# Scaling the forgetting-attention probabilities on GpSimd in place of ScalarE

## The chip, the core and the metric

The kernel runs on one core of a Trainium2 chip. A core has four engines that matter here: TensorE (PE in the profile, with its weight loads as PEld), VectorE (DVE), ScalarE (ACT) and GpSimd (POOL). A fifth, SyncE (SP), issues most DMAs. Each engine works through its own queue strictly in order and waits on semaphores for the others. The metric is the device time of one execution in microseconds (us), lower is better; what is compared is the median of several executions.

## What is computed

Two decoder layers, each: half a SwiGLU feed-forward, a token mixer, another half feed-forward. 512 tokens, model width 1024. The mixer has eight forgetting-attention (FoX) heads of width 64 and four differential-attention heads. For one block of 128 queries the FoX heads compute

```python
s_f = einsum('bhqd,bhkd->bhqk', qf, k_f) * scale_f
s_f = s_f + cf[..., :, None] - cum_f[..., None, :]
s_f = where(causal, s_f, -inf)
p_f = softmax(s_f, axis=-1)
o_f = einsum('bhqk,bhkd->bhqd', p_f, v_f)
```

The last step of that softmax is a division of each row by its sum. This is the step that the change touches.

## The kernel before, in words

**Precision.** Matrix products run in a split form: an operand is stored as a rounded high part and a low remainder, and three products replace one. `split` (lines 82 to 85) makes the parts: ScalarE copies the high part (L83), VectorE subtracts it from the source (L84). Both engines therefore work for TensorE throughout the program.

**The mixer.** Its attention is a list of twelve units, four differential heads and then eight FoX heads, each cut into four query blocks. The loop over `s` in `mixer` is a software pipeline: at step `s` it emits the softmax of one query block (`softmax_step`), the transposes of the probabilities of a unit five steps behind (`trans_step`), and the product with V six steps behind (`pv_step`). Between those, `fill_to` emits pieces of matrix products that do not depend on attention (projections for later heads, then the early part of the output projection); the table `TARGET` says how much filler has been emitted by each unit. The table runs flat toward the end, so the last FoX heads have little filler beside them.

**One FoX query block**, with `n` keys (128, 256, 384 or 512), goes through these lines:

1. TensorE computes the scores into PSUM (L821, L822) and adds the causal mask (L824).
2. VectorE adds the forget-gate row from a tile named `rope` in the profile (its buffer is reused), writes the result `e` into the probability tile `pg`, and takes the row minimum into `st` (L857). The signs are flipped, so the minimum plays the part of a maximum.
3. ScalarE computes the exponential in place and the row sum (L859, followed by a read of the accumulator).
4. VectorE takes the reciprocal of the row sum (L860), 128x1.
5. ScalarE multiplies the block in place by that reciprocal (L861).
6. TensorE transposes the probabilities (L871); ScalarE and VectorE split them into the two parts (L880, L881, tiles `pair` and `pt`); TensorE multiplies by V (L910, L911); ScalarE copies half of the result (L940, `fot`) and VectorE adds the other half (L941); L892 and L893 split the result into `y` for the output projection.

There are two `pg` tiles, one for even units and one for odd ones, so a unit's probabilities are overwritten two units later.

**Other work at the same time.** ScalarE and VectorE also split the keys and queries of the next heads (L770, L771, L758, L759, from `kdup` and `qk_t`), the output-projection weights into `XA` (L83, L84), and evict projections (L787).

**GpSimd** issues DMAs that add one weight block onto another (L134) in the feed-forward stages, casts a table once per mixer (L626), and multiplies four tiles at the very end of the program (L1144).

**What sets the order.** The code is written as one program; a scheduler walks it and gives each engine a fixed sequence, with its own estimate of how long each instruction takes. A change of engine for one operation can therefore move its neighbours.

Of the kernel before, what the change touches and what calls it, by code (L numbers as in the profile page):

```python
# [12 lines left out]
ALU = mybir.AluOpType  # L13
# [39 lines left out]
def trunk(ctx, tc, xT, x, gains, gain_row, w_gu, w_dn, w_in, w_ff, w_out, fbias, lams, subln, consts, rope, out):  # L53
    nc = tc.nc
    act, dve, pool, pe, sp = nc.scalar, nc.vector, nc.gpsimd, nc.tensor, nc.sync
# [524 lines left out]
    def mixer(l, n_next, mid):  # L580
# [14 lines left out]
        def pr_tile(u, qb):  # L595
            w = (qb + 1) * P
            return pg[u % 2][:, PR[qb]:PR[qb] + w]

        def pm_tile():
            return pg[nxt("pm", 2)][:, 1280:1792]  # L600
# [215 lines left out]
        def scores(q1, kk, m, qb, masked):  # L816
            n = (qb + 1) * P
            w = max(n, 256)
            p = psum("b")
            lq = q1[m][:, qb * P:n]  # L820
            pe.matmul(p[:, 0:w], lq, kk[m][:, 0, 0:w], start=True, stop=False)  # L821
            pe.matmul(p[:, 0:w], lq, kk[m][:, 1, 0:w], start=False, stop=not masked)  # L822
            if masked:
                pe.matmul(p[:, qb * P:n], identb, maskb, start=False, stop=True)  # L824
            return p
# [3 lines left out]
        def softmax_step(u, qb):  # L829
            kind, h = units[u]  # L830
            n = (qb + 1) * P
            st = sm.tile([P, 6], F32, tag="st", name="st", bufs=6)
            if kind == "d":
                q1, kk = qk[("d", h)]
                pm = []
                for m in range(2):
                    p = scores(q1, kk, m, qb, False)
                    e = pr_tile(u, qb) if m == 0 else pm_tile()
                    dve.tensor_tensor_reduce(out=e[:, 0:n], in0=p[:, 0:n], in1=maskw[:, S - n:S], op0=ALU.add,
                                             op1=ALU.min, scale=1.0, scalar=3.0e38, accum_out=st[:, m:m + 1])  # L840
                    act.activation(out=e[:, 0:n], in_=e[:, 0:n], func=AF.Exp, scale=-1.0, bias=st[:, m:m + 1],
                                   accum_out=st[:, 2 + m:3 + m])
                    pm.append(e)
                dve.reciprocal(out=st[:, 4:6], in_=st[:, 2:4])
                dve.tensor_tensor(out=st[:, 5:6], in0=st[:, 5:6], in1=nlam, op=ALU.mult)
                act.mul(out=pm[1][:, 0:n], in_=pm[1][:, 0:n], mul=st[:, 5:6])
                dve.scalar_tensor_tensor(out=pm[0], in0=pm[0], scalar=st[:, 4:5], in1=pm[1][:, 0:n],
                                         op0=ALU.mult, op1=ALU.add)
                probs[u].append(pm[0])
            else:  # L850
                q1, kk = qk[("f", h // 2)]
                if qb == 0:
                    cbs[h] = rope_t[h % 2]
                    sp.dma_start(out=cbs[h], in_=cum_d[h:h + 1, :].partition_broadcast(P))
                p = scores(q1, kk, h % 2, qb, True)
                e = pr_tile(u, qb)
                dve.tensor_tensor_reduce(out=e, in0=p[:, 0:n], in1=cbs[h][:, 0:n], op0=ALU.add, op1=ALU.min,  # L857
                                         scale=1.0, scalar=3.0e38, accum_out=st[:, 0:1])
                act.activation(out=e, in_=e, func=AF.Exp, scale=-1.0, bias=st[:, 0:1], accum_out=st[:, 2:3])  # L859
                dve.reciprocal(out=st[:, 4:5], in_=st[:, 2:3])  # L860
                act.mul(out=e, in_=e, mul=st[:, 4:5])  # L861
                probs[u].append(e)

        pts = {}
# [216 lines left out]
        for s in range(4 * len(units) + 5 + LAG):  # L1081
            u, i = divmod(s, 4)

            def pace(j):
                a = target[min(u, len(target) - 1)]
                b = target[min(u + 1, len(target) - 1)]
                fill_to(a + (b - a) * (3 * i + j) / 12)
            now, later[:] = list(later[:1]), later[1:]
            v, kb = divmod(s - 4 - LAG, 4)
            if 0 <= v < len(units):  # L1090
                trans_step(v, kb)
            pace(1)
            if u < len(units):
                softmax_step(u, i)
            pace(2)
            for f in now:
                f()
            v, kb = divmod(s - 5 - LAG, 4)
            if 0 <= v < len(units):
                pv_step(v, kb)  # L1100
            pace(3)
# [250 lines left out]
```

## Time and profile before

| | |
|---|---|
| median of 3 executions | 1886.66 us (1884.94 to 1890.23) |
| the profiled execution | 1887.3 us, of which the span from first to last instruction is 1885.2 us |
| mean granted TensorE clock | 0.992 of full speed |
| ScalarE busy over the whole span | 1139.6 us, 60% |
| VectorE busy | 1625.6 us, 86% |
| GpSimd busy | 129.0 us, 7% |
| FoX blocks, both mixers | 64, first L861 at 486.7 us, last at 1506.9 us |
| the multiplies at L861 alone | 387 to 737 ns, median 560 ns |

The profile gives each engine's busy time over the span and in windows of it, the groups of instructions by line, who waited for whom, and the chain of work that ended last, followed backwards from the end. The first mixer's FoX blocks run their multiplies from 486.7 to 582.1 us, the second mixer's from 1411.6 to 1506.9 us; the two stretches look alike, shifted by about 925 us. TensorE's busy time is modelled from pipelined matmuls, so overlapping matmuls count as busy even where the pace is lower; its weight-load time is the better measure of how much work it was given in a stretch.

### The profile page before, as it was taken

How to read it: one execution, taken by the hardware profiler on the slowest of the kernel's cores; microseconds unless marked ns; L12 is line 12 of the kernel's file. 1: busy time of each engine (PE TensorE's matmuls, PEld its weight loads, DVE VectorE, ACT ScalarE, POOL GpSimd, SP SyncE). 2: the span in 40 equal slices, each digit the busy share in tenths (PEclk: the TensorE clock that was granted, in tenths of full speed). 3: DMA queues.
4: the chain of work that ended last, by engine and by line, in shares of the span. 5: the costliest groups of instructions: out<-in, count | busy, mean ns of one | idle time of the engine just before them, and what ended most of it. 6: DMA issues, size and time to landing. Idle time of an engine off the chain costs nothing.

```text
span 1885.2 us, 24722 instructions
## 1 busy us (share of the span) xinstructions
PE 1837.5 (97%) x8814; PEld 1511.2 (80%) x8814; DVE 1625.6 (86%) x2537; ACT 1139.6 (60%) x1797; POOL 129.0 (7%) x156
## 2 busy tenths in 40 slices
PE   7999999999999999999999999999999999999997
PEld 5788888787877889888878988887788688888886
DVE  7799998878685989899998989997786869998988
ACT  6565546546786755565585556554577957455564
POOL 2000000000000000000001000000000000000101
PEclk8999999999999999999999999999999999999999
DMA  9676675243336576676647666643433367756842
GB/s 298 185 208 183 188 193 150 69 135 106 100 115 195 168 193 175 160 213 181 180 140 218 173 173 181 173 140 99 125 102 108 111 178 197 212 143 184 226 111 90
DMA packets 95962, 305.38 MB, mean 162 GB/s; under 512 B 12616, under 2 KB 15176, under 8 KB 95840
## 3 DMA queue, kind: packets, MB, share of 16 engines
q1 hardware_dynamic: 74960, 232.68, 36.7%
q0 software_dynamic: 19584, 69.21, 20.6%
q10 hardware_dynamic: 1296, 1.93, 0.3%
q8 instruction: 69, 1.13, 0.2%
q14 instruction: 53, 0.43, 0.1%
HBM read 289.03 MB, written 2.16 MB: 154 GB/s over the span
## 4 chain that ended last, share of the span: by engine, by line
PE 81%; DVE 10%; ACT 5%; DMA 2%; issue 1%; SPq 0%; DVEq 0%; ACTq 0%
PE ps_c L385 12%; PE ps_c L386 12%; PE ps_c L387 12%; PE ps L386 9%; PE ps L385 9%; PE ps L387 9%; PE ps_a L385 3%; PE ps_a L386 3%; PE ps_a L387 3%; DVE wg L84 3%; PE ps_t L487 2%; DVE x L516 1%; ACT pg L859 1%; DMA raw<-w_gu 1%; PE ps_b L871 1%
## 5 line engine op out<-in xcount | busy, mean ns | idle before, releaser
L83 ACT CAST wg<-raw 128x1024 fp32r<-128x1024 f32 (+1 forms) x533 | 545.2, 1030 | 492.0 <-PE ps_c L387 183.0
L84 DVE TENSOR_TENSOR wg<-raw,wg 128x1024 fp32r<-128x1024 f32 (+1 forms) x533 | 629.7, 1192 | 111.2 <-ACT wg L83 108.1
L385 PE MATMUL ps_c<-wg,xf 128*128 128x512 f32 (+1 forms) x768 | 287.6, 375 | 3.8 <-ACT xf L83 1.6
L386 PE MATMUL ps_c<-wg,xf 128*128 128x512 f32 (+1 forms) x768 | 286.4, 373 | 1.8 <-DVE wg L84 1.8
L387 PE MATMUL ps_c<-wg,xf 128*128 128x512 f32 (+1 forms) x768 | 284.9, 373 | 0.0
L385 PE MATMUL ps<-wg,xf 128*128 128x512 f32 (+1 forms) x576 | 219.2, 382 | 7.4 <-ACT wg L83 7.3
L386 PE MATMUL ps<-wg,xf 128*128 128x512 f32 (+1 forms) x576 | 216.2, 376 | 0.6 <-DVE wg L84 0.6
L387 PE MATMUL ps<-wg,xf 128*128 128x512 f32 (+1 forms) x576 | 215.1, 375 | 1.2 <-DVE xf L84 1.2
L385 PEld LDWEIGHTS ps_c<-wg,xf 128*128 128x128 f32 x768 | 145.3, 189 | 31.8 <-ACT xf L83 2.8
L386 PEld LDWEIGHTS ps_c<-wg,xf 128*128 128x128 f32 x768 | 145.6, 190 | 27.4 <-DVE wg L84 2.7
L387 PEld LDWEIGHTS ps_c<-wg,xf 128*128 128x128 f32 x768 | 144.9, 189 | 25.3 <-DVE xf L84 0.4
L134 POOL DMA_DIRECT2D raw<-w_gu x88 | 76.4, 868 | 1131.9 <-DMA raw<-w_gu 667.6
L385 PE MATMUL ps_c<-wg,hf 128*128 128x512 f32 x352 | 138.6, 394 | 4.4 <-DVE x L516 4.3
L386 PE MATMUL ps_c<-wg,hf 128*128 128x512 f32 x352 | 137.5, 391 | 0.0
L387 PE MATMUL ps_c<-wg,hf 128*128 128x512 f32 x352 | 137.3, 390 | 0.0
L385 PEld LDWEIGHTS ps<-wg,xf 128*128 128x128 f32 x576 | 110.1, 191 | 25.9 <-ACT wg L83 7.8
L387 PEld LDWEIGHTS ps<-wg,xf 128*128 128x128 f32 x576 | 109.6, 191 | 20.9 <-DVE xf L84 1.7
L386 PEld LDWEIGHTS ps<-wg,xf 128*128 128x128 f32 x576 | 110.1, 191 | 18.9 <-DVE wg L84 1.1
L516 DVE SCALAR_TENSOR_TENSOR x<-ps_c,x 128x512 f32<-128x512 f32 x192 | 124.3, 684 | 1.0 <-PE ps_c L387 0.9
L385 PE MATMUL ps_a<-XA,wg 128*128 128x512 f32 x256 | 106.9, 418 | 2.6 <-ACT XA L339 1.9
L386 PE MATMUL ps_a<-XA,wg 128*128 128x512 f32 x256 | 101.9, 398 | 2.5 <-DVE XA L340 2.5
L386 PE MATMUL ps<-wg,hf 128*128 128x512 f32 x264 | 103.2, 391 | 0.0
(274 smaller groups left out, 3516.1 us busy)
## 6 DMA issues: line engine op xcount, KB each, us to landing
raw<-w_gu SPq DMA_DIRECT2D x219, 512.0 KB, 4.3
raw<-w_dn SPq DMA_DIRECT2D x100, 512.0 KB, 3.6
raw<-w_gu POOLq DMA_DIRECT2D x88, 512.0 KB, 7.3
raw<-w_in SPq DMA_DIRECT2D x48, 512.0 KB, 3.4
raw<-w_dn POOLq DMA_DIRECT2D x40, 512.0 KB, 5.7
kdup<-qk_t SPq DMA_DIRECT2D x64, 128.0 KB, 2.3
raw<-w_out SPq DMA_DIRECT2D x16, 512.0 KB, 3.7
raw<-w_dn SPq DMA_DIRECT2D x20, 256.0 KB, 3.4
```

What stands on the lines that cost most here:

```text
L83: act.copy(out=hi, in_=src)
L84: dve.tensor_tensor(out=lo, in0=src, in1=rf(hi), op=ALU.subtract)
L134: pool.dma_start(out=t, in_=where(two, h)[1], accum_op=ALU.add)
L385: pe.matmul(p, lh, rh, start=start, stop=False, skip_group_check=again)
L386: pe.matmul(p, lh, rl, start=False, stop=False, skip_group_check=again)
L387: pe.matmul(p, ll, rh, start=False, stop=stop, skip_group_check=again)
L487: pe.transpose(pj[j][:, e * 256 + p * P:e * 256 + (p + 1) * P], hs[j][p][:, o:o + P], ident)
L516: dve.scalar_tensor_tensor(out=xc, in0=src, scalar=scale, in1=xc, op0=ALU.mult, op1=ALU.add)
L859: act.activation(out=e, in_=e, func=AF.Exp, scale=-1.0, bias=st[:, 0:1], accum_out=st[:, 2:3])
L871: pe.transpose(p[:, (qb - kb) * P:(qb - kb + 1) * P], probs[u][qb][:, kb * P:(kb + 1) * P], ident)
```

## The change

The in-place multiply of a FoX block by its reciprocal row sum leaves ScalarE and becomes a tensor-scalar multiply on GpSimd. The differential heads keep theirs (L846) on ScalarE. Nothing else in the source is edited.

```diff
 act.activation(out=e, in_=e, func=AF.Exp, scale=-1.0, bias=st[:, 0:1], accum_out=st[:, 2:3])
 dve.reciprocal(out=st[:, 4:5], in_=st[:, 2:3])
-act.mul(out=e, in_=e, mul=st[:, 4:5])
+pool.tensor_scalar(out=e, in0=e, scalar1=st[:, 4:5], scalar2=None, op0=ALU.mult)
 probs[u].append(e)
```

The scheduler moves other instructions with it, in the two FoX stretches only. On ScalarE, in the last FoX heads of the first mixer (`pg_2961` and `pg_2962` are the probability tiles of even and odd units), this stood in its queue before:

```order
L861 ACTIVATE pg_2962<-pg_2962,st 128x512
L859 ACTIVATE pg_2961,st<-pg_2961,st 128x128
L880 CAST pair<-ps_b 128x512
L861 ACTIVATE pg_2961<-pg_2961,st 128x128
L859 ACTIVATE pg_2961,st<-pg_2961,st 128x256
L940 COPY fot<-ps_b 64x512
L880 CAST pair<-ps_b 128x384
L859 ACTIVATE pg_2961,st<-pg_2961,st 128x384
L861 ACTIVATE pg_2961<-pg_2961,st 128x256
L880 CAST pair<-ps_b 128x256
```

and for the same head this stands there now:

```order
L859 ACTIVATE pg_2961,st<-pg_2961,st 128x128
L880 CAST pair<-ps_b 128x512
L859 ACTIVATE pg_2961,st<-pg_2961,st 128x256
L940 COPY fot<-ps_b 64x512
L880 CAST pair<-ps_b 128x384
L83 CAST XA_2950<-raw 128x1024
L880 CAST pair<-ps_b 128x256
L83 CAST XA_2955<-raw 128x1024
L859 ACTIVATE pg_2961,st<-pg_2961,st 128x384
L859 ACTIVATE pg_2961,st<-pg_2961,st 128x512
```

The multiplies are gone from between the exponentials and the splits, and two casts of the output-projection weights have come up into this head from later ones.

On GpSimd, around the first mixer, the queue held only the table cast and the weight DMAs before:

```order
L626 CAST tri<-tri_f 128x512
L134 DMA raw<-w_dn 128x1024
L134 DMA raw<-w_gu 128x1024 x8
L134 DMA raw<-w_dn 128x1024
L134 DMA raw<-w_gu 128x1024
```

Now the 32 multiplies of the eight FoX heads stand between; these are the last of them, with the DMAs of the next feed-forward behind:

```order
L861 TENSOR_SCALAR pg_2961<-pg_2961,st 128x512
L861 TENSOR_SCALAR pg_2962<-pg_2962,st 128x128
L861 TENSOR_SCALAR pg_2962<-pg_2962,st 128x256
L861 TENSOR_SCALAR pg_2962<-pg_2962,st 128x384
L861 TENSOR_SCALAR pg_2962<-pg_2962,st 128x512
L134 DMA raw<-w_gu 128x1024 x8
```

The DMAs of the next feed-forward stage now wait in line behind the last multiply.

On VectorE, in the last heads of the first mixer, the queue around the third `XA` split was before:

```order
L857 ISA pg_2961,st<-ps_b,rope 128x256
L857 ISA st 128x1
L84 TENSOR_TENSOR XA_2950<-raw,XA_2950 128x1024
L860 RECIPROCAL st<-st 128x1
L857 ISA pg_2961,st<-ps_b,rope 128x384
L857 ISA st 128x1
L881 TENSOR_TENSOR pair<-ps_b,pair 128x512
L860 RECIPROCAL st<-st 128x1
L941 TENSOR_TENSOR pg_2961<-ps_b,fot 64x512
```

and is now:

```order
L857 ISA pg_2961,st<-ps_b,rope 128x256
L857 ISA st 128x1
L84 TENSOR_TENSOR XA_2950<-raw,XA_2950 128x1024
L860 RECIPROCAL st<-st 128x1 x3
L857 ISA pg_2961,st<-ps_b,rope 128x384
L857 ISA st 128x1
L941 TENSOR_TENSOR pg_2961<-ps_b,fot 64x512
L84 TENSOR_TENSOR XA_2955<-raw,XA_2955 128x1024
L881 TENSOR_TENSOR pair<-ps_b,pair 128x512
```

Three reciprocals, which were spread out, now stand together behind the `XA` split, and the next `XA` split follows closely.

## The prediction

> **What bounds the kernel now.** I read the page first, for the share of each engine and the chain of work that ended last.
>
> ```profile
> PE 1837.5 (97%) x8814; PEld 1511.2 (80%) x8814; DVE 1625.6 (86%) x2537; ACT 1139.6 (60%) x1797; POOL 129.0 (7%) x156
> PE 81%; DVE 10%; ACT 5%; DMA 2%; issue 1%; SPq 0%; DVEq 0%; ACTq 0%
> ```
>
> Over the span TensorE is the bound, and ScalarE is only 60% busy. Taking work from it is worth nothing unless there is a place where it is late. The chain has 5% ScalarE, so I looked for that place with busy times by stage around the FoX heads.
>
> ```profile
> 486.00:540.00 54.00, 54.00 (x277) 43.60 (x276) 36.62 (x85) 38.39 (x76) 0.00 (x0) 1.00 0.31 98
> 540.00:560.00 20.00, 19.21 (x107) 14.45 (x105) 18.84 (x56) 19.11 (x48) 0.00 (x0) 1.00 0.51 146
> 560.00:580.00 20.00, 17.43 (x92) 12.71 (x93) 16.22 (x47) 19.84 (x50) 0.00 (x0) 1.00 0.18 60
> 1465.00:1485.00 20.00, 19.02 (x106) 14.40 (x104) 18.93 (x55) 19.13 (x48) 0.00 (x0) 1.00 0.52 146
> 1485.00:1505.00 20.00, 17.60 (x93) 12.87 (x94) 16.04 (x46) 19.84 (x51) 0.00 (x0) 1.00 0.19 64
> ```
>
> Behind the length of a window stand PE, PEld, DVE, ACT and POOL busy. From 486 to 540 us TensorE never stops: filler covers every wait, and the FoX multiplies there are worth nothing. From 540 to 580 us ScalarE is busy 19.11 + 19.84 = 38.95 of 40 us. **This stretch is bound by ScalarE.** The second mixer repeats it (38.97 of 40 us).
>
> What else would need time there? VectorE is busy 18.84 + 16.22 = 35.06 us, so it has 4.94 us left. For TensorE I use weight loads: at its saturated pace it does 43.60 us of them in 54 us, so the 14.45 + 12.71 = 27.16 us take 27.16 x 54 / 43.60 = 33.6 us, and it has 6.4 us left. VectorE stands closest behind ScalarE.
>
> **What the change removes.** ScalarE's rows in 540 to 580 us:
>
> ```profile
> L859 ACT ACTIVATE pg<-pg,st 128x512 f32<-128x512 f32 (+3 forms) x20 | 11.2, 560 | 0.0
> L861 ACT ACTIVATE pg<-pg,st 128x512 f32<-128x512 f32 (+3 forms) x20 | 11.1, 561 | 0.0
> ```
>
> Twenty multiplies, 11.1 us, leave ScalarE: 38.95 - 11.1 = 27.9 of 40 us. ScalarE is then no bound at all, and what is late next is VectorE. The most that the stretch can lose is therefore VectorE's 4.94 us, not 11.1. How much of that idle time did ScalarE cause? VectorE's waits in the same stretch:
>
> ```profile
> DVE st L860 <- ACT pg L859: 0.7, 2, 0.5
> DVE XA L84 <- ACT XA L83: 0.7, 1, 0.7
> DVE pg L857 <- PE ps_b L824: 0.5, 2, 0.3
> DVE pt L881 <- ACT pt L880: 0.5, 1, 0.5
> DVE pair L881 <- ACT pair L880: 0.5, 2, 0.3
> DVE pg L941 <- ACT fot L940: 0.4, 1, 0.4
> DVE qk L771 <- ACT qk L770: 0.3, 1, 0.3
> DVE y L893 <- ACT y L892: 0.2, 1, 0.2
> ```
>
> Seven of the eight are on ScalarE: 0.7 + 0.7 + 0.5 + 0.5 + 0.4 + 0.3 + 0.2 = 3.3 us. I take these 3.3 us as what VectorE wins, because a ScalarE with 30% of its time free is seldom the late one; VectorE would then be busy 35.06 / 36.7 = 96%. The ends are 4.94 us (VectorE never idle) and 0 (its waits come back in another form).
>
> **What it adds on GpSimd.** No row of before has this multiply at its widths. The nearest rows:
>
> ```profile
> L1144 POOL TENSOR_TENSOR x<-x,gr 128x512 f32<-128x512 f32 x4 | 5.1, 1287 | 27.0 <-ACT sq L1119 27.0
> L626 POOL CAST tri<-tri_f 128x512 fp32r<-128x512 f32 x2 | 1.2, 615 | 9.0 <-DMA tri_f<-consts 9.0
> L1205 POOL TENSOR_SCALAR ngains<-gains_sb 128x56 f32<-128x56 f32 x1 | 0.4, 354 | 2.0 <-DMA gains_sb<-gains 2.0
> ```
>
> The multiply has one tensor input, as L626 and L1205 have. A line through these two gives (615 - 354) / 456 = 0.57 ns a column, so 395, 468, 542 and 615 ns at the four widths and a mean of 0.51 us, about ScalarE's 0.56. That is the value I take; the upper end is the two-input row, 1.29 us at any width. GpSimd has 40 / 20 = 2.0 us per multiply in the stretch, so it is not a bound at either end, and the latency of a block changes little. Behind the last multiply in GpSimd's queue stand the weight DMAs of the next feed-forward:
>
> ```profile
> 592.42 0.86 POOL L134 DMA_DIRECT2D raw<-w_gu  x1 [263.82 <-DMA raw<-w_gu]
> ```
>
> The first of them starts at 592.42 us, held by another DMA, and the last multiply of before started at 582.1 us. These 10 us cover the queueing: cost 0. If the cover were gone, each us of lateness would delay that DMA by a us.
>
> **The toll on VectorE.** The end of the program shows GpSimd and VectorE side by side:
>
> ```profile
> 1869.68 5.06 POOL L1144 TENSOR_TENSOR x<-x,gr 128x512 f32<-128x512 f32 x4 [27.05 <-ACT sq L1119]
> ...
> 1872.97 0.69 DVE L516 SCALAR_TENSOR_TENSOR x<-ps_c,x 128x512 f32<-128x512 f32 x1 [0.53 <-PE ps_c L387]
> 1873.58 1.18 DVE L1124 TENSOR_TENSOR fst<-fst 128x2 f32<-128x2 f32 x1
> ...
> 1876.40 0.16 DVE L1124 TENSOR_TENSOR fst<-fst 128x2 f32<-128x2 f32 x1
> ```
>
> L1124, two columns with both inputs in SBUF, lasts 1.18 us when it meets the last GpSimd multiply and ends at 1874.76, when GpSimd ends (1874.74); alone it lasts 0.16. So it stood still for 1.0 us. L516, which reads PSUM and one SBUF tile, keeps its 0.69 us inside the GpSimd run. I conclude that a VectorE operation with two SBUF inputs waits for a running GpSimd operation and that others don't. The Trainium skill, GPSIMD Engine Reference, section "Specifications", speaks against this change with the same words: GpSimd's SBUF interfaces are shared with VectorE, with contention for VectorE instructions that have two SBUF inputs or run in a two-port mode. The trace agrees (1.18 against 0.16 us).
>
> How many such operations has the stretch? These:
>
> ```profile
> L84 DVE TENSOR_TENSOR XA<-raw,XA 128x1024 fp32r<-128x1024 f32 x4 | 4.9, 1216 | 0.8 <-ACT XA L83 0.7
> L771 DVE TENSOR_TENSOR qk<-kdup,qk 128x512 fp32r<-128x512 f32 x4 | 2.8, 690 | 0.5 <-ACT qk L770 0.3
> L893 DVE TENSOR_TENSOR y<-pg,y 128x512 fp32r<-128x512 f32 x3 | 2.1, 688 | 0.2 <-ACT y L892 0.2
> L759 DVE SCALAR_TENSOR_TENSOR qk<-qk_t,qk 64x512 fp32r<-64x512 f32 x2 | 1.4, 686 | 0.1
> L893 DVE TENSOR_TENSOR y<-ou,y 128x512 fp32r<-128x512 f32 x1 | 0.7, 681 | 0.0
> ```
>
> Fourteen, 11.9 us; L857 and L881 read PSUM and go free. GpSimd runs 20 x 0.51 = 10.2 of 40 us, so 14 x 0.26 = 3.6 of them meet a multiply and wait half of it, 0.26 us: 0.9 us. With 1.29 us each GpSimd runs 65% of the time: 14 x 0.65 x 0.64 = 5.8 us; the lower end is 0. I take 1.1 us, a little over the middle value, since the new order puts three reciprocals together and their multiplies run into the next XA split.
>
> **The sum.** Per mixer 3.3 - 1.1 = 2.2 us, twice 4.4 us. The profiled execution took 1887.3 us: 1882.9. It lies 0.6 us above the median of 1886.66; I predict for the median, 1882.5 us. A measurement of this kernel can tell about 0.3% from no change, here 5.7 us; the forecast lies inside that.
>
> **The rivals.**
>
> *ScalarE's relief goes all the way.* VectorE loses its 4.94 us of idle time and pays next to no toll: 1887.3 - 9.9 = 1877.4 us. For it: casts come up in ScalarE's queue, so VectorE's sources are ready early. Against: VectorE is already at 18.84 of 20 us in 540 to 560, where it can hardly win.
>
> *A wait takes the place of the one removed.* TensorE's waits in the stretch:
>
> ```profile
> PEld ps_b L910 <- ACT pair L880: 2.9, 5, 1.1
> PEld ps_b L871 <- ACT pg L861: 1.8, 4, 1.2
> PE ps_b L910 <- ACT pair L880: 1.7, 2, 0.9
> ```
>
> The waits on L861 would become waits on GpSimd, which must itself wait for VectorE's reciprocal (now queued behind the 1.2 us XA split) and for the shared interface; those on L880 become waits on VectorE. The 2.2 us go: about 1887 us. Against: only 1.8 us of these waits were on the multiply, and the pipeline leaves five steps between a softmax and its transposes.
>
> *The toll eats more than the relief: slower.* Place: VectorE from 540 to 580 us. Every multiply then blocks VectorE for its whole length, by alternating with its two-input operations or because PSUM readers pay too: 20 x 0.51 = 10.2 us per mixer against 3.3 won, 6.9 us lost, twice 13.8: 1901 us. With half of that toll it is 1887.3 + 3.6 = 1891. It decides from 3.3 / 20 = 0.17 us lost per multiply. Against: L516's 0.69 us. The Trainium skill, on the same page and section, names two-port modes as a second kind of VectorE instruction that contends; no row here shows whether L857 or L860 run in one.
>
> *The change not doing what it says* is no separate case: GpSimd is at 0.00 us in all these windows.
>
> **How the numbers follow.** Forecast, small gain near 1882.5 (1879 to 1885.5): 0.50. Relief all the way, near 1877.5: 0.23. New wait, near 1887: 0.15. Toll, 1889 to 1901: 0.12. Faster by over 0.3% means under 1881.0: nearly all of the second case and a quarter of the first, 0.35. Slower by over 0.3%, above 1892.3, takes most of the last case and some tail of the third, 0.12. Within: 0.53. The range runs from under the relief case to the half toll: 1876 to 1891.
>
> **What would show it.** In the new profile, ScalarE should be near 28 of 40 us in the last FoX heads and VectorE at 95% or more; the waits of L910 on L880 should shrink; multiplies of 0.4 to 0.65 us on GpSimd; L84 and L771 sometimes 0.1 to 0.5 us longer, L857 and L881 unchanged; the feed-forward that follows unchanged and only shifted. The prediction is wrong if VectorE's idle time in the stretch stays near 5 us, or if L857 or L881 become longer.

## The result and the profile after

| | before | after |
|---|---|---|
| median of 6 executions each | 1887.53 us (1884.94 to 1890.23) | 1899.90 us (1897.62 to 1900.45) |
| ratio to before | | 1.0062, 95% interval [1.0051, 1.0073] |
| span of the profiled execution | 1885.2 us | 1895.8 us |

The change makes the kernel 0.62% slower, some 12 us. The forecast of 1882.5 us was wrong, and so was its range, which ended at 1891.

From the page of the changed kernel, the busy times and the chain that ended last:

```profile
PE 1837.7 (97%) x8814; PEld 1512.3 (80%) x8814; DVE 1624.3 (86%) x2537; ACT 1113.5 (59%) x1733; POOL 206.8 (11%) x220
...
PE 83%; DVE 10%; ACT 3%; DMA 2%; POOL 1%; issue 1%; SPq 0%; DVEq 0%; ACTq 0%; POOLq 0%
```

The page hardly shows the loss. ScalarE gave up 26 us, GpSimd took up 78, and GpSimd appears on the chain with 1%. TensorE's busy share stays at 97%, because 10 us more of waiting is half a per cent of the span. The windows over the FoX heads show it. Behind the length of a window stand PE, PEld, DVE, ACT and POOL busy, then the granted clock:

```profile
486.00:540.00 54.00, 51.73 (x263) 41.27 (x262) 36.08 (x85) 33.41 (x68) 12.77 (x11) 1.00 0.35 109
540.00:560.00 20.00, 16.62 (x91) 12.40 (x89) 16.24 (x48) 15.78 (x37) 10.58 (x8) 1.00 0.25 77
560.00:580.00 20.00, 16.56 (x85) 12.72 (x86) 14.32 (x40) 12.40 (x30) 8.62 (x9) 0.91 0.32 101
...
1485.00:1505.00 20.00, 15.09 (x73) 11.09 (x72) 13.82 (x40) 12.32 (x32) 8.98 (x8) 0.89 0.36 106
1505.00:1525.00 20.00, 18.80 (x98) 14.58 (x98) 14.43 (x35) 11.57 (x26) 9.10 (x7) 0.94 0.52 169
```

ScalarE fell to 15.78 + 12.40 = 28.2 of 40 us, nearly to the microsecond what was forecast. But nothing rose in its place: VectorE fell from 35.06 to 30.56 us and TensorE from 36.64 to 33.18. Even from 486 to 540 us, where TensorE had not stopped at all, 2.3 us are idle. **All engines together became idler**: the sign of a chain that goes from engine to engine and waits for its own latency, not of an engine that has too much work. The waits from 540 to 580 us name the link:

```profile
POOL pg L861 <- DVE st L860: 22.0, 9, 4.6
PEld ps_b L871 <- POOL pg L861: 7.2, 6, 2.0
ACT pair L880 <- PE ps_b L871: 7.0, 6, 2.2
PE ps_b L871 <- POOL pg L861: 5.2, 6, 1.7
DVE pair L881 <- ACT pair L880: 4.9, 5, 1.7
```

Read downwards, this is one relay: GpSimd waits for a reciprocal, TensorE's transposes (L871) wait for GpSimd, ScalarE's split waits for the transposes, VectorE's split waits for ScalarE. The two rows of TensorE are the price: 12.4 us in this stretch, where before the same transposes waited for the multiply 2.7 us in both rows together. Over 486 to 600 us they are 20.8 us (12.1 + 8.7); PE and PEld wait partly at the same time, so this sum compares kernels and is not lost time itself.

All of it is for the two widest blocks of a head: 15.7 us for those of 512 columns, 5.1 us for those of 384, nothing for 128 and 256. These have the longest multiplies and the least room. By the loop over `s`, the first transposes of unit `u` come at step `4u + 5` and read the first 128 columns of all four blocks, whose softmax was emitted at steps `4u` to `4u + 3`. So the five steps of the description lie between the first block and the transposes; the 512-column block has two.

The multiplies on GpSimd, by shape (busy time, then mean ns of one):

```profile
L861 POOL TENSOR_SCALAR pg<-pg,st 128x512 f32<-128x512 f32 x16 | 27.5, 1720 | 44.4 <-DVE st L860 44.4
L861 POOL TENSOR_SCALAR pg<-pg,st 128x384 f32<-128x384 f32 x16 | 21.5, 1347 | 49.6 <-DVE st L860 39.7 <-PE ps_a L664 9.3 <-PE ps_a L385 0.6
L861 POOL TENSOR_SCALAR pg<-pg,st 128x256 f32<-128x256 f32 x16 | 17.4, 1090 | 23.5 <-DVE st L860 19.2 <-PE ps_b L871 2.4 <-ACT pair L880 1.8
L861 POOL TENSOR_SCALAR pg<-pg,st 128x128 f32<-128x128 f32 x16 | 11.7, 732 | 329.7 <-DVE st L860 329.7
```

Their mean is (1720 + 1347 + 1090 + 732) / 4 = 1222 ns, against 560 on ScalarE and 510 in the prediction. And they come in bunches. GpSimd's timeline, runs of multiplies with the idle time ahead of each in brackets:

```profile
557.39 4.57 POOL L861 TENSOR_SCALAR pg<-pg,st 128x384 f32<-128x384 f32 x4 [4.63 <-DVE st L860]
566.57 1.24 POOL L861 TENSOR_SCALAR pg<-pg,st 128x384 f32<-128x384 f32 x1 [4.61 <-DVE st L860]
```

GpSimd stands idle for 4.6 us, then has four blocks in a row, and the last of them is ready 4.6 us after the run began.

Where the time went: from the first matmul of the V projections (L662) to the end of the last output addition (L990), 230.3 us became 237.2 in the first mixer (+7.0) and 229.3 became 237.3 in the second (+8.0). Together that is 15.0 us, of which 4.4 came back elsewhere in the two profiled executions, 3.1 of them ahead of the first mixer, where no instruction was changed; that part stays unexplained and is within what executions of one kernel differ by.

### The profile page after: what moved, and what is told of

It reads as the page before. It is cut to its first block, busy times and chain, and to the rows that moved or that the text cites. A ratio compares the mean times of both kernels' runs of the same rounds, so it can differ in the third digit from the quotient of the medians.

```text
span 1895.8 us, 24874 instructions
## 1 busy us (share of the span) xinstructions
PE 1837.7 (97%) x8814; PEld 1512.3 (80%) x8814; DVE 1624.3 (86%) x2537; ACT 1113.5 (59%) x1733; POOL 206.8 (11%) x220
## 4 chain that ended last, share of the span: by engine, by line
PE 83%; DVE 10%; ACT 3%; DMA 2%; POOL 1%; issue 1%; SPq 0%; DVEq 0%; ACTq 0%; POOLq 0%
PE ps_c L385 12%; PE ps_c L386 12%; PE ps_c L387 12%; PE ps L386 9%; PE ps L385 8%; PE ps L387 8%; PE ps_a L385 3%; PE ps_a L387 3%; PE ps_a L386 3%; DVE wg L84 3%; PE ps_t L487 2%; POOL pg L861 1%; DVE x L516 1%; PE ps_b L871 1%; DVE hf L84 1%
## 5 line engine op out<-in xcount | busy, mean ns | idle before, releaser
L84 DVE TENSOR_TENSOR wg<-raw,wg 128x1024 fp32r<-128x1024 f32 (+1 forms) x533 | 628.4, 1189 | 110.4 <-ACT wg L83 108.8
L861 POOL TENSOR_SCALAR pg<-pg,st 128x128 f32<-128x128 f32 (+1 forms) x64 | 77.8, 1222 | 447.3 <-DVE st L860 433.1
L385 PE MATMUL ps_a<-XA,wg 128*128 128x512 f32 x256 | 106.0, 414 | 2.4 <-ACT XA L339 1.9
L134 POOL DMA_DIRECT2D raw<-w_dn x48 | 41.6, 866 | 574.9 <-DVE wg L84 228.9
```

What stands on the lines that cost most here:

```text
L84: dve.tensor_tensor(out=lo, in0=src, in1=rf(hi), op=ALU.subtract)
L134: pool.dma_start(out=t, in_=where(two, h)[1], accum_op=ALU.add)
L385: pe.matmul(p, lh, rh, start=start, stop=False, skip_group_check=again)
L861: pool.tensor_scalar(out=e, in0=e, scalar1=st[:, 4:5], scalar2=None, op0=ALU.mult)
```

## The experiments

Three explanations had to be told apart; the third was a term of the prediction's own sum. **Length** (the first expectations call it the price): a block's multiply takes too long, wherever it stands in the queues. **Order**: the sequence that the scheduler now gives the engines is worse, whatever engine multiplies. **Toll**: GpSimd slows VectorE over the shared SBUF interface.

Most kernels below pin one of the two sequences. A table holds the instruction numbers of the two FoX stretches in the sequence of before or of after, engine by engine, and each instruction is tied to the one ahead of it by an edge that costs no wait:

```diff
+    traced = {i.name: i for i in nc.cur_bb.bb.instructions}
+    for names in ORDER:
+        q = [traced[n] for n in (f"I-{k}" for k in names) if n in traced]
+        for a, b in zip(q, q[1:]):
+            tc.add_manual_dep(b, a.name, mybir.DependencyInfo(
+                mybir.DependencyClass.NoSync, mybir.DependencyReason.DATA), reason="order")
...
```

The multiply itself is not in the tables; its place among the others of its engine is the scheduler's choice. All ratios are to the kernel before, measured beside each kernel, with 95% intervals.

### Engine and order apart

The multiply on GpSimd, in the order of before:

```diff
-act.mul(out=e, in_=e, mul=st[:, 4:5])
+pool.tensor_scalar(out=e, in0=e, scalar1=st[:, 4:5], scalar2=None, op0=ALU.mult)
...
+ORDER = [...]    # sequence of before
```

> The multiplies are on GpSimd, and TensorE, VectorE, ScalarE and SyncE keep the order that they had before the change. Price theory (a GpSimd multiply lasts 1.2 us where ScalarE's lasted 0.56, and TensorE stands at the transposes that wait for it): 1895 to 1910 us, as slow as the change or slower. Order theory (the scheduler's new order does the harm, not the multiply): within 3 us of before, or up to 5 us faster. Toll theory (GpSimd holds up VectorE's operations with two SBUF inputs): about 1900 us, and VectorE's L84, L771, L893 longer than before.

The multiply on ScalarE, in the order of after:

```diff
 act.mul(out=e, in_=e, mul=st[:, 4:5])
...
+ORDER = [...]    # sequence of after
```

> The multiplies are back on ScalarE, and TensorE, VectorE, SyncE and the rest of ScalarE keep the order that came with the change. Price theory: within 4 us of before (1884 to 1892). Order theory: about 1900 us, as the change. Toll theory: as before.

| median us, ratio to before | order of before | order of after |
|---|---|---|
| multiply on ScalarE | the kernel before | 1888.38, 1.0006 [0.9997, 1.0015] |
| multiply on GpSimd | 1889.10, 1.0009 [1.0000, 1.0019] | 1899.90, 1.0062 [1.0051, 1.0073] |

Neither alone costs more than 0.2%; only the two together cost 0.62%. No theory of a single cause survives this table. GpSimd's timeline and TensorE's waits (486 to 600 us) in the order of before:

```profile
549.02 1.25 POOL L861 TENSOR_SCALAR pg<-pg,st 128x384 f32<-128x384 f32 x1 [1.81 <-PE ps_b L824]
551.57 1.57 POOL L861 TENSOR_SCALAR pg<-pg,st 128x512 f32<-128x512 f32 x1 [1.31 <-DVE st L860]
...
568.72 0.60 POOL L861 TENSOR_SCALAR pg<-pg,st 128x128 f32<-128x128 f32 x1 [0.85 <-DVE st L860]
570.06 0.93 POOL L861 TENSOR_SCALAR pg<-pg,st 128x256 f32<-128x256 f32 x1 [0.73 <-DVE st L860]
```

```profile
PEld ps_b L871 <- POOL pg L861: 4.2, 6, 1.2
PE ps_b L871 <- POOL pg L861: 2.3, 5, 0.9
```

Here the multiplies come mostly one at a time, about a microsecond apart, and the transposes wait 6.5 us for them instead of 20.8. The four undisturbed lengths, 0.60, 0.93, 1.25 and 1.57 us at 128, 256, 384 and 512 columns, lie on a line: 0.28 us and 2.52 ns a column.

### More room, and half of the heads

The transposes one step further behind the softmax, the rest as in after:

```diff
-LAG = 1
+LAG = 2
```

> The change, with the transposes emitted one step later behind their softmax (LAG 2 in place of 1), so that each multiply has about 2 us more. Price theory: most of the loss is won back, 1884 to 1892 us, and TensorE's waits on L861 go from 20.8 us a mixer to under 6. Toll theory: no change, 1897 to 1902, since VectorE and GpSimd do the same work at the same time. Order theory says nothing sure, because the order changes again.

Measured 1891.20 us, 1.0017 [1.0008, 1.0027]: nearly 9 of the 12 us come back. TensorE's waits on L861 from 486 to 600 us are 9.6 us instead of 20.8 (under 6 was expected), all of them for 512-column blocks. This kernel has an order of its own, so it supports latency as the cause without proving it.

Only the last five FoX heads on GpSimd:

```diff
+if h >= 3:
     pool.tensor_scalar(out=e, in0=e, scalar1=st[:, 4:5], scalar2=None, op0=ALU.mult)
+else:
+    act.mul(out=e, in_=e, mul=st[:, 4:5])
```

> Only FoX heads 3 to 7 (those with little filler beside them) multiply on GpSimd, heads 0 to 2 on ScalarE. Price theory with cover by filler: nearly the whole loss stays, 1896 to 1901. If the first three heads carry a share by their number (3 of 8), 1895. Order theory: no fixed value; toll theory: 1896 to 1900, as most VectorE operations with two SBUF inputs stand beside the last heads.

Measured 1890.89 us, 1.0013 [1.0004, 1.0023]. All expectations missed, also the one that gave the first three heads a share by their number. Part of the loss lies in the first three, as the window of 486 to 540 us of after shows (51.73 of 54 us); and this kernel too has an order of its own.

### The length of the operation

An operation that is short on GpSimd in place of the multiply, once in each order:

```diff
-pool.tensor_scalar(out=e, in0=e, scalar1=st[:, 4:5], scalar2=None, op0=ALU.mult)
+pool.tensor_copy(out=e, in_=e)
```

> The order that came with the change, GpSimd instruction for instruction at the same place, but a plain in-place copy in place of the multiply (the FoX probabilities stay unscaled). Length theory (the loss is the length of the GpSimd multiply, 0.6 to 1.7 us): the copy lasts 0.3 to 0.6 us and the time falls to 1880 to 1887 us, where the blind sum of this document had put it with that length. Hand-over theory (a third engine in the chain and its semaphores cost the time, whatever the instruction): it stays at 1897 to 1901.

> As before the change in the order of TensorE, VectorE, ScalarE and SyncE, with a plain in-place copy on GpSimd at the place of the multiply (the FoX probabilities stay unscaled). Length theory: 2 to 8 us under before, 1880 to 1886. Hand-over theory: about 1889, as the multiplies in this order gave.

Measured 1879.06 us, 0.9951 [0.9933, 0.9969], in the order of after, and 1884.90, 0.9984 [0.9974, 0.9993], in that of before. The order that costs 0.62% with the multiply gains 0.49% with the copy, which takes 482 to 768 ns (means of the four widths). But the copy also doesn't wait for the reciprocal. So the next kernels keep the multiply, its waits and the order of after, and shorten it alone. The columns that it leaves out don't wait for GpSimd any more, but the first transpose of every block reads columns 0 to 127, part or all of which the short multiply still writes:

```diff
-pool.tensor_scalar(out=e, in0=e, scalar1=st[:, 4:5], scalar2=None, op0=ALU.mult)
+pool.tensor_scalar(out=e[:, 0:n // 4], in0=e[:, 0:n // 4], scalar1=st[:, 4:5], scalar2=None, op0=ALU.mult)
```

> The order that came with the change, the multiply on GpSimd behind the same reciprocal, but only on the first quarter of each block's columns (32 to 128 in place of 128 to 512; the other columns stay unscaled). Every wait and hand-over is kept, only the length shrinks, to 0.36 to 0.60 us. Length theory: 1879 to 1886 us. Hand-over theory (the trip VectorE to GpSimd to TensorE): 1893 to 1900.

The same with `n // 2`:

> The order that came with the change, the multiply on GpSimd on the first half of each block's columns (64 to 256 columns, 0.44 to 0.92 us; the rest stays unscaled). If lengths only add up: half way between the quarter (1881.2) and the whole (1899.9) by length, about 1888. If the new order has room up to a length and then tips over: nearer to the quarter, 1881 to 1885.

And the quarter in the order of before:

> The order of before, the multiply on GpSimd on the first quarter of each block's columns (0.36 to 0.60 us; the rest stays unscaled). With the whole multiply this order gave 1889.1, with a copy 1884.9. Expected 1883 to 1887: this order gains little from a short multiply and loses little from a long one.

| columns multiplied | mean length, order of after | ratio | mean length, order of before | ratio |
|---|---|---|---|---|
| a quarter | 0.64 us | 0.9961 [0.9949, 0.9973] | 0.59 us | 0.9980 [0.9970, 0.9990] |
| a half | 0.82 us | 0.9995 [0.9986, 1.0005] | | |
| all | 1.22 us | 1.0062 [1.0051, 1.0073] | 1.18 us | 1.0009 [1.0000, 1.0019] |

**This settles the main point.** With engine, order and waits alike, the length of the multiply moves the result from a gain to a loss, and the three points lie on a line: 0.0034 over 0.19 us, then 0.0067 over 0.40 us, about 1.8% and 1.7% for each microsecond of length. In the order of before it is 0.0029 over 0.59 us, 0.5% for a microsecond. The new order makes the kernel three to four times as sensitive to the length (at least twice, with the intervals at their ends). TensorE's waits on L861 (486 to 600 us) and a window of the quarter kernel show the relief that was forecast:

```profile
PEld ps_b L871 <- POOL pg L861: 3.1, 7, 1.1
PE ps_b L871 <- POOL pg L861: 1.2, 2, 0.9
```

```profile
560.00:580.00 20.00, 18.67 (x105) 14.35 (x104) 18.21 (x51) 14.87 (x36) 5.68 (x9) 1.00 0.42 143
```

The transposes wait 4.3 us, ScalarE is at 14.87 of 20 us, and VectorE at 18.21 has become the next bound.

### The operation by itself

Extra operations on a scratch tile at the start of the kernel before, where GpSimd has nothing else to do:

```diff
+for n in (128, 256, 384):
+    pool.tensor_scalar(out=gh[:, 0:n], in0=gh[:, 0:n], scalar1=ngains[:, 0, 0:1], scalar2=None, op0=ALU.mult)
+for n in (128, 384):
+    pool.tensor_scalar(out=gh[:, 0:n], in0=gh[:, 0:n], scalar1=0.5, scalar2=None, op0=ALU.mult)
+for n in (128, 384):
+    pool.tensor_copy(out=gh[:, 0:n], in_=gh[:, 0:n])
```

> The kernel before with eight extra GpSimd instructions at the start, where VectorE stands idle: a multiply by a column of scalars at 128, 256 and 384 columns, a multiply by a constant at 128 and 384, a copy at 128 and 384. Length theory: multiplies by a column 0.60, 0.92, 1.24 us alone, so that the length is the instruction's own and not contention. Toll theory: 0.40, 0.47, 0.54 us alone (the line through the two rows of before), the rest being contention.

The groups of these instructions, and VectorE's timeline at the time of the first:

```profile
L1209 POOL TENSOR_SCALAR gh<-gh,ngains 128x384 f32<-128x384 f32 x1 | 2.3, 2310 | 0.1
...
L1209 POOL TENSOR_SCALAR gh<-gh,ngains 128x256 f32<-128x256 f32 x1 | 0.9, 922 | 0.1
L1209 POOL TENSOR_SCALAR gh<-gh,ngains 128x128 f32<-128x128 f32 x1 | 0.6, 602 | 0.1
L1213 POOL COPY gh<-gh 128x384 f32<-128x384 f32 x1 | 0.5, 507 | 0.1
...
L1213 POOL COPY gh<-gh 128x128 f32<-128x128 f32 x1 | 0.3, 329 | 0.1
```

```profile
5.35 0.69 DVE L84 TENSOR_TENSOR wg<-raw,wg 128x512 fp32r<-128x512 f32 x1 [5.35 <-ACT wg L83]
5.96 0.68 DVE L84 TENSOR_TENSOR xf<-bt,xf 128x512 fp32r<-128x512 f32 x1
```

The multiply costs (922 - 602) / 128 = 2.5 ns a column, the copy (507 - 329) / 256 = 0.70. A line through a cast and a multiply, as the prediction drew it, mixes two operations; the slopes of copy and multiply differ by a factor of 3.6. The Trainium skill, GPSIMD Engine Reference, section "4.1 Engine selection", calls one-input operations on GpSimd roughly line-rate; the copy bears that out (ScalarE's multiply takes (737 - 387) / 384 = 0.9 ns a column) and the multiply by a column doesn't, so the measurement decides. The 384-column multiply, which ran while VectorE did its two L84 operations, took 2.31 us instead of 1.25, and VectorE's kept their 0.69 us: in this meeting GpSimd paid.

### The toll on VectorE

The kernel before with a multiply on GpSimd added behind each reciprocal, on a scratch tile that nobody reads, at most 384 columns wide:

```diff
 act.mul(out=e, in_=e, mul=st[:, 4:5])
+pool.tensor_scalar(out=gh[:, 0:min(n, 384)], in0=gh[:, 0:min(n, 384)], scalar1=st[:, 4:5], scalar2=None, op0=ALU.mult)
```

> The kernel before, with its multiplies on ScalarE and its order unchanged, and besides 64 multiplies on GpSimd on a scratch tile, each behind the same reciprocal (128, 256, 384 and again 384 columns), whose results nobody reads. Toll theory (GpSimd holds up VectorE): 1895 to 1900 us, and L84, L771, L893 longer. Length theory: within 3 us of before, since nobody waits for them.

Measured 1887.66 us, 1.0000 [0.9990, 1.0010]. VectorE's two-input groups from 540 to 580 us, and some of the added work over the whole span:

```profile
L86 DVE TENSOR_TENSOR XA<-raw,XA 128x1024 fp32r<-128x1024 f32 x4 | 4.9, 1214 | 0.8 <-ACT XA L85 0.8
L773 DVE TENSOR_TENSOR qk<-kdup,qk 128x512 fp32r<-128x512 f32 x4 | 2.8, 711 | 0.1
```

```profile
L864 POOL TENSOR_SCALAR gh<-gh,st 128x384 f32<-128x384 f32 x32 | 42.6, 1333 | 84.3 <-DVE st L862 84.1
```

These are L84 and L771 of before, where they lasted 1216 and 690 ns. GpSimd works 70 us here, VectorE's operations between the first and the last reciprocal of a stretch add up to 0.4 us more, and the kernel loses nothing.

This was the order of before. For the order of after the traces of after and of the kernel with the multiply on ScalarE can be compared: the same 188 VectorE operations, in the same sequence, take 84.9 us in place of 84.5 in each mixer. The toll theory is refuted as a cause of the loss.

**Most of the toll falls on GpSimd.** Of the 64 multiplies of after, 33 met no VectorE operation with two SBUF inputs, and these lasted what the line 0.28 us + 2.52 ns a column gives, within 0.01 us. The 15 that began while such an operation had more than 0.3 us to run all lasted 0.26 to 1.07 us longer, 8.9 us together, which is the whole difference between 1.22 and 1.09 us in the mean. The other way round, 17 such VectorE operations began inside a multiply that had more than 0.3 us to run: 13 kept their length within 0.03 us, and four lasted 0.23 to 0.37 us longer; three of the four had begun within 0.2 us of the multiply's start.

### Why the new order is so sensitive: a miss

In after, several reciprocals stand together behind an L84 split. I took that queue for the cause of the bunches and moved four splits of each mixer behind the reciprocals that follow them (shown is the one ahead of three; the others stood ahead of one or two):

```diff
 ORDER = [...]    # sequence of after, on VectorE:
-L84 XA, L860, L860, L860
+L860, L860, L860, L84 XA
```

> The change with one thing moved in VectorE's order: four weight splits (L84, 1.2 us each) per mixer that stand directly ahead of reciprocals go behind them. Queue theory (in the new order reciprocals come late and in a row, so that multiplies of 0.6 to 1.7 us stand in line on GpSimd): about half of the loss goes, 1890 to 1896, and the time from reciprocal to multiply shrinks little, that from exponential to reciprocal by some 0.2 us. If only the sum of lengths counts: 1898 to 1901.

Measured 1903.92 us, 1.0086 [1.0063, 1.0108], no faster than after (1.0062; the intervals overlap), where 1890 to 1896 was expected. The theory fell. For the last five heads, the mean time from the end of an exponential to its reciprocal did shrink, from 0.87 to 0.61 us, but from the reciprocal to the multiply it stayed 0.7 us, and the bunches stayed too:

```profile
561.25 5.03 POOL L861 TENSOR_SCALAR pg<-pg,st 128x384 f32<-128x384 f32 x4 [4.66 <-DVE st L860]
```

The bunches are seen in the traces; that they make the sensitivity, and what makes them, wasn't shown. Taking one engine's sequence from before and the others' from after was not tried.

### Versions that might win

The kernel before with three casts of the splits (L770, L892 and those of `XA`) on GpSimd, as copies are cheap there:

```diff
-act.copy(out=k_[:, 0], in_=dup)
+pool.tensor_copy(out=k_[:, 0], in_=dup)
...
-act.copy(out=oh, in_=u)
+pool.tensor_copy(out=oh, in_=u)
...
-return split(got[0], w[:, 0:1024], w[:, 1024:2048])
+pool.tensor_copy(out=w[:, 0:1024], in_=got[0])
+dve.tensor_tensor(out=w[:, 1024:2048], in0=got[0], in1=rf(w[:, 0:1024]), op=ALU.subtract)
+return w[:, 0:1024], w[:, 1024:2048]
```

> The kernel before, multiplies on ScalarE, but three other kinds of ScalarE work of the FoX stretch on GpSimd: the copies of L770 (from kdup), L892 (y) and the XA casts of L83 (8.5 us of ScalarE's 39 in the stretch). A GpSimd copy lasts 0.70 ns a column where a multiply by a column lasts 2.5 (bench), so 0.62 us at 512 and about 1.0 at 1024 columns, as on ScalarE. Relief theory: ScalarE falls to 30 of 40 us, the stretch loses 2 to 4 us a mixer, 1879 to 1884. If GpSimd's place in the chain itself costs: 1887 or more.

Measured 1885.10 us, 0.9990 [0.9978, 1.0002]: no change that can be told from none, and between the two expectations. ScalarE is busy 34.1 of 40 us there, so it was relieved by less than half of what the multiplies take.

The multiply on GpSimd only where it is short there:

```diff
+if n <= 256:
     pool.tensor_scalar(out=e, in0=e, scalar1=st[:, 4:5], scalar2=None, op0=ALU.mult)
+else:
+    act.mul(out=e, in_=e, mul=st[:, 4:5])
```

> Blocks of 128 and 256 columns multiply on GpSimd (0.60 and 0.92 us), those of 384 and 512 on ScalarE; order by the scheduler. Length theory: ScalarE loses 4.5 of 11.1 us per stretch, the waits of TensorE on GpSimd stay near 5 us a mixer; 1884 to 1891, near before.

Measured 1878.61 us, 0.9951 [0.9933, 0.9969], better than expected. The same kernel (`pool_narrow`) once more, in more rounds:

> The kernel of pool_narrow again, with more rounds: 1876 to 1881, 0.4 to 0.6% under before.

Measured 1877.82 us, **0.9944 [0.9931, 0.9956]**: faster than both kernels. The same split of the blocks in the order of before:

> Blocks of 128 and 256 columns multiply on GpSimd, TensorE, VectorE and SyncE in the order of before. If the gain of pool_narrow is the engine's (ScalarE relieved of 4.5 us, by multiplies of 0.60 and 0.92 us): 1878 to 1883. If it came from the order that the scheduler gave it: 1885 to 1889.

Measured 1885.01 us, 0.9986 [0.9977, 0.9995]. So a quarter of the gain is there without a new order, and the larger part comes with the order that this kernel gets. Its windows, and TensorE's waits on the multiply from 486 to 600 us (L874 and L864 are L871 and ScalarE's L861 here):

```profile
540.00:560.00 20.00, 18.64 (x105) 13.86 (x103) 18.41 (x52) 19.63 (x48) 4.42 (x5) 1.00 0.42 115
560.00:580.00 20.00, 20.00 (x118) 16.10 (x117) 18.99 (x50) 18.81 (x44) 5.81 (x6) 1.00 0.53 168
...
1485.00:1505.00 20.00, 20.00 (x112) 15.76 (x112) 17.55 (x43) 17.51 (x42) 4.69 (x4) 1.00 0.51 170
```

```profile
PEld ps_b L874 <- ACT pg L864: 1.8, 4, 0.9
PE ps_b L874 <- ACT pg L864: 0.5, 1, 0.5
```

All three engines are well used at once: TensorE no longer stops from 560 to 580 us, where it lost 2.6 us before and 3.4 after. It never waits for GpSimd's multiplies: the 384- and 512-column blocks, for which it waited 20.8 us in after, are ScalarE's again, and the blocks that moved have four or five steps of room. No run with this order and the wide blocks on GpSimd was made, so how much of the gain this choice makes is not shown.

## Why the prediction was wrong, step by step

**ScalarE as the bound of the stretch, and its relief: right.** ScalarE came out at 28.2 of 40 us, "near 28" as forecast. That the relief is worth something, and that VectorE comes next, holds where the multiply is short: the quarter kernel, whose multiplies would last 0.48 us undisturbed by the line above and last 0.64 in place, gains 0.39%, some 7 us, where the sum said 4.4 us for 0.51 us. So in the new order the relief was sized too small; in the old one the same short multiply gains 0.20%, about 4 us. (The sum itself has a slip: 1886.66 - 4.4 is 1882.3, not 1882.5.)

**The step that failed is the multiply on GpSimd**, in the paragraph "What it adds on GpSimd": "about ScalarE's 0.56. That is the value I take". It measured 1.22 us in after, 1.09 undisturbed. The line ran through a 512-column cast and a 56-column multiply; copies cost 0.70 ns a column, multiplies by a column 2.5. The upper end of 1.29 us held as a mean, though not "at any width": the widest blocks took 1.72.

**The inference from that length failed too**: "it is not a bound at either end, and the latency of a block changes little". The first half is true, GpSimd is busy 19.2 of 40 us. The second is not. Throughput was priced, latency was given nothing, so even the correct length would have entered the sum only through the toll. The runs put 1.7 to 1.8% on each microsecond of length in this order: from 0.51 to 1.22 us that is an estimated 1.2 to 1.3%, or 23 to 24 us, with the line extended a little below its shortest point of 0.64. Against the forecast gain this is more than the whole miss of 17 us (1899.9 against 1882.5).

**The rival "a wait takes the place of the one removed" had the mechanism and the place.** It named TensorE's waits on L861, on GpSimd, behind VectorE's reciprocal and its `XA` split. It was priced at 2.2 us, the loss of the gain, and argued down with the five steps between a softmax and its transposes. Five is right for the 128-column block alone; the 512-column block, with the longest multiply, has two, and three quarters of the waits are for it. Nor are steps a time: the scheduler orders by its own estimate of lengths. The waits grew from 2.7 to 20.8 us a mixer. The new queues that I showed as three reciprocals together went into the sum only as part of the toll.

**The toll on VectorE was sized too large and put on the wrong engine**: 1.1 us a mixer in the sum, 0.4 measured, while the multiplies on GpSimd became 8.9 us longer over both mixers. Among the rivals it was nearly the only way to a slower kernel, and its price of 1901 us, within 2 us of the measured 1899.9, is a hit by luck. `XA` splits lasted 1224 ns and L771 692 (1216 and 690 before), and with 64 idle multiplies beside it the kernel lost nothing. The exception in this window are two L759, 874 ns instead of 686:

```profile
L84 DVE TENSOR_TENSOR XA<-raw,XA 128x1024 fp32r<-128x1024 f32 x4 | 4.9, 1224 | 0.0
...
L771 DVE TENSOR_TENSOR qk<-kdup,qk 128x512 fp32r<-128x512 f32 x4 | 2.8, 692 | 1.3 <-ACT qk L770 1.2
...
L759 DVE SCALAR_TENSOR_TENSOR qk<-qk_t,qk 64x512 fp32r<-64x512 f32 x2 | 1.7, 874 | 0.1
```

The 1.18 us of L1124 was read from a single row, and the conclusion that every VectorE operation with two SBUF inputs waits for a running GpSimd operation went too far: 13 of 17 did not.

**Of the signs named in advance**, ScalarE's 28 us came true, and L857 and L881 kept their lengths (681 and 692 ns at 512 columns). The waits of L910 on L880 did shrink, from 2.9 us to 0.2 in PEld's row, probably because the transposes ahead of them were late. VectorE at 95% did not come, and multiplies under 0.65 us only at 128 columns (0.60). "VectorE's idle time stays near 5 us" was given as the sign of a wrong prediction; it was 9.4.

**What stays open**: why the new order turns the length into lost time three to four times as strongly as the old. TensorE's own queue gives no clear answer. From the last scores of a head to the transpose that reads its 512-column block, 49 matmuls stood in the third head before and 30 stand there now, in the eighth 31 and 20; but in the sixth and seventh it is the other way, 23 and 29, 21 and 27.

## What to carry to other kernels

When a step of a pipeline moves to an idle engine, price its latency and not only that engine's load: how much later is each block ready, and who stands waiting at the head of a strictly ordered queue. Ask it block by block: the version that won moved only the blocks for which TensorE had not waited. Measure the very operation, at its widths and in two sizes, since operations of one engine differ by more than three times per column, and a line through two kinds is no estimate. When a scheduler makes a new order with the move, test the engine with the old order and the order with the old engine before blaming either.

## What the hardware showed that I had not expected

- On GpSimd, in fp32 and SBUF, a multiply by a per-partition column takes 0.28 us + 2.52 ns a column, a copy 0.70 ns a column.
- Where GpSimd's multiplies and VectorE's operations with two SBUF inputs met, GpSimd mostly paid: all 15 multiplies that began during such an operation became longer, and 13 of 17 VectorE operations that began during a multiply did not.
- The clock fell after much waiting. In after, from 558 to 572 us, TensorE is busy 9.42 of 14 us, and the window after it ran at 0.57 of the clock:

```profile
558.00:572.00 14.00, 9.42 (x51) 6.70 (x50) 10.18 (x27) 8.56 (x22) 6.74 (x6) 1.00 0.40 111
572.00:576.00 4.00, 3.92 (x12) 2.98 (x12) 1.83 (x4) 1.16 (x3) 3.22 (x4) 0.57 0.62 218
```

A 512-column matmul took 0.63 us there instead of 0.39. The means of 0.91 (560 to 580 us) in the first mixer, 0.89 (1485 to 1505) and 0.94 (1505 to 1525) in the second cost 1.8 and 3.4 us at full work, which is at the most a quarter of the first mixer's loss of 7.0 us and some two fifths of the second's 8.0. The clock alone doesn't make the loss: the multiply on GpSimd in the order of before also has 0.91 from 560 to 580 us, and its ratio is 1.0009. The Trainium skill, TensorE: Matmul & The Clock Gate, section "Part 1: The HAM clock gate", has the clock fall to half after an idle window of about 3.4 us; the fall is there, but no wait on L861 was longer than 2.0 us, TensorE was busy 1.61 us in the 3.41 us ahead of the fall (568.74 to 572.15 us), and no run was made to see which pattern of idle time sets it off.
